# First layer's attention in fixed ticks, four projection blocks moved beside the memory, ten k-tiles of the output projection beside the attention

## Chip, cores and metric

One core of a Trainium2 chip runs the whole program in one launch. The metric is the device time of that launch in microseconds (us). TensorE (PE) multiplies and transposes, VectorE (DVE), ScalarE (ACT) and GpSimd (POOL) do the elementwise work, and SyncE (SP) issues nearly all DMAs from one queue. Each engine works through its own instructions in order and waits on semaphores for the others, so an instruction that waits also holds up everything behind it on its engine.

## The reference, cut to what matters

Two layers, 1280 tokens of width 1024 (1024 sample tokens, 256 prompt tokens). The first layer runs two mixers on one input projection:

```python
qa, ka, va, za, qb, kb, vb, ob, zb, gb = jnp.split(h @ w_in, AB_SPLITS, axis=-1)
# A: 16 heads on 4 key heads, window +-128 (sample) plus 256 cached keys, a sink logit per head
s_loc = jnp.einsum('bqhgd,bkhd->bhgqk', qi, ki) * scale      # 3 blocks of 128 keys, masked
s_ctx = jnp.einsum('bqhgd,bkhd->bhgqk', qi, ck) * scale      # 256 cached keys
p = jax.nn.softmax(jnp.concatenate([s_loc, s_ctx, sink_b], axis=-1), axis=-1)
a_out = attn * jax.nn.silu(za)
# B: matrix memory, chunkwise, both directions, 4 heads
hb, states = _mlstm_bidir(qb, kb, vb, ob, gb + gate_bias, conv_w, norm_w, init)
b_out = hb * jax.nn.silu(zb)
out = jnp.concatenate([a_out, b_out], axis=-1) @ w_out       # 16 k-tiles of 128
```

The second layer (latent attention) follows; the change does not alter what it computes.

## The kernel before, in words

Every matmul operand is split into a high and a low part (names ending in h and l), and each product is three matmuls: high by high, high by low, low by high. The first layer's input projection is cut into 30 blocks of 256 columns (`DenseBlock`). A block's weights come in four DMAs of two k-tiles each into `wf` (two buffers); `split` then casts each k-tile to `wh` on ACT (L350) and subtracts on POOL to get `wl` (L351). A block is about ten cost units of 24 matmuls each for 256 columns, two units for 512.

The order of the work is set in two ways. Outside a `manual_schedule` block a scheduler with a timing model orders each engine's instructions. Inside, the order is that of the code. `beside_memory` is of the second kind: the memory's work is cut into 80 visits of 2 slots each, 174 slots in all, and every slot issues the steps of `Visit.STEPS` for the visits that are due, then dense work up to a quota (`while spent * slots < (s + 1) * total`), then one call of `dense.pump`, which either asks for a DMA of the next block's weights or splits weights that came at least three slots after the last ask. When a block starts, `load` asks and splits at once whatever is still missing. Steps that must come later in the flow are put off by `K.later`.

The stages of the first layer: five blocks while the gates are made, 20 blocks beside the memory, then attention. Attention has 4 key groups `g` by 10 query blocks `b`. `a_attn` makes the scores of four heads in the PSUM tile `D`, takes the maximum on DVE, the exponential on ACT and the normalisation on POOL (`att_p`). `a_use` turns each block of 128 keys with four PE transposes into `T`, splits it into `att_ph` (ACT) and `att_pl` (DVE), and multiplies by the values into `V`. I call one key block of `a_use` a turn; there are 168. The first 21 of the 40 groups stand beside the last five dense blocks, the others beside `out_tile` of 9 token tiles, with 12 of the 16 k-tiles of the output projection (`woh`, `wol`, `o_ah`, `o_al`); a tenth token tile follows. The remaining 4 k-tiles come in a second pass, `wo2`, with the norm for the second layer.

Of the kernel before, what the change touches and what calls it, by code (L numbers as in the profile page):

```python
# [77 lines left out]
class Kern:  # L78
    def __init__(self, tc, I, O, dbg):
        self.tc, self.nc, self.I, self.O, self.dbg = tc, tc.nc, I, O, dbg  # L80
        self.uid = 0
        self.flow = self.ring = None

# [245 lines left out]
class DenseBlock:  # L329


    def __init__(self, K, wp, cols, fn, bufs, width, src="w_in_ab"):
        self.K, self.wp, self.cols, self.fn, self.bufs, self.width = K, wp, cols, fn, bufs, width
        self.src, self.w, self.wf, self.asked = K.I[src][0], [], [], 0
# [26 lines left out]
    def run(self):  # L361

        units = self.fn(self.w)
        if self.K.flow:
            for half in range(2):
                for u in units[0:2]:
                    u.products(half)
                    yield u.cost / 2
            units = units[2:]
        for u in units:  # L370
            for half in range(2):
                u.products(half)
                if half or u.cost > 1:
                    yield min(u.cost, 1)


class Unit:
# [8 lines left out]
    def products(self, half):  # L386
        K = self.K
        if not half:
            self.ps = K.ps()
        for k in range(half * KD // 2, (half + 1) * KD // 2):  # L390
# [4 lines left out]
        if half:  # L395
            self.done(self.ps)

# [24 lines left out]
class Dense:  # L422
# [162 lines left out]
def rope_split(K, pool, ps, t0, N, scale, dh, dl):  # L585
# [4 lines left out]
    nc.vector.tensor_mul(t, ps[:, 0:N], tab[:, 0, t0:t0 + N])  # L590
    nc.vector.stream_shuffle(s, ps[:, 0:N], ROT16)
    nc.gpsimd.tensor_mul(s, s, tab[:, 1, t0:t0 + N])

    def add():
        nc.vector.tensor_add(t, t, s)
        split_to(K, pool, t, 128, N, scale, dh, dl)

    K.later(add)
# [39 lines left out]
def layer_ab(K):  # L638
# [97 lines left out]

    K.set_psum(S=3, mm=3, T=2)
    bp = left("mls")
    with K.tc.manual_schedule():
        beside_memory(K, bp, dense, 20, 200)  # L740
    bp.release()
    K.set_psum(D=2, mm=1, V=1, T=2)
    ap = left("att")
    a_sinks(K, ap)
    attn = pipelined([a_attn(K, ap, g) for g in range(4)], 2)
    banks = itertools.cycle((partial(K.bank, "mm"), K.psT, K.psT))

    def beside(n):

        K.ps = lambda: next(banks)()  # L750
        for i, cost in enumerate(dense.stream(5)):
            if i == n:
                del K.ps
            yield cost

    weave(attn, 21, beside(10), 50, 0)
    K.rpool.release()
    tp.release()
    K.ring = None
    wp.release()  # L760
    hp.release()
    p = right("wo1")
    w = I["w_out_ab"][0]
    ks = [8, 9, 10, 11, 12, 13, 14, 15, 0, 1, 2, 3]
    wt = load_wout(K, p, w, ks)
    K.y1 = [K.t(K.dram, [128, D], F32, f"y1_{t}") for t in range(NT)]
    K.y2 = [K.t(K.dram, [128, D], F32, f"y2_{t}") for t in range(NT)]
    gate = gate_rows(K, p, 0)

    def first_part(tts):  # L770
        for tt in tts:
            srcs = [(d["bT"][tt], 0, 6), (d["bT"][tt], 6, 8, d["aT"][tt], 0, 4)]
            K.dma(K.y1[tt], out_tile(K, p, srcs, wt, gate[0 if tt < 8 else 1], x_src(K, tt), 6))
            yield 1

    weave(attn, 4 * NT + 1 - 21, first_part(range(9)), 9, 7)
    K.ps = lambda: next(banks)()
    for _ in first_part(range(9, NT)):
        pass
    p.release()  # L780
    ap.release()
    gp.release()
    del K.ps
    K.set_psum(S=5, T=3)
    p = left("wo2")
    wt = load_wout(K, p, w, range(4, 8))
# [10 lines left out]
    for tt in range(NT):  # L797
        if tt in (0, 8):
            gate = gate_row(K, p, 0, tt // 8)
        y = out_tile(K, p, [(d["aT"][tt], 4, 8)], wt, gate, K.y1[tt], 4, xb=2)  # L800
# [10 lines left out]
def load_wout(K, p, src, ks):  # L811

    nc = K.nc
    stage = [K.t(p, [128, D], F32, "o_y", 2) for _ in range(2)]
    out = [[p.tile([128, D], F32R, tag=f"{t}{i}", name=K.nm(t)) for t in ("woh", "wol")] for i in range(len(ks))]
    for i, (k, (wh, wl)) in enumerate(zip(ks, out)):
        wf = stage.pop(0) if stage else K.t(p, [128, D], F32, "o_y", 2)
        K.dma(wf, src[k * 128:(k + 1) * 128, :])
        nc.scalar.copy(wh, wf)
        (nc.gpsimd if i % 3 else nc.vector).tensor_sub(wl, wf, wh.bitcast(F32))  # L820
# [3 lines left out]
def out_tile(K, p, srcs, wt, gate, res, nk, each=None, xb=1, fast=False):  # L824
# [4 lines left out]
    y = K.t(p, [128, D], F32, "o_y", 2)  # L829
# [122 lines left out]
def a_attn(K, ap, g):  # L952
    nc, d = K.nc, K.d
    j, r = g // 2, (g % 2) * 64
    kk = []
    for nm in ("kh", "kl"):
        t = K.t(ap, [128, 1536], F32R, "att_" + nm, 1)
        for half in range(2):
            K.dma(t[half * 64:half * 64 + 64, :], d[nm][j][r:r + 64, :])
        kk.append(t)  # L960
    kkh, kkl = kk
    VA = K.t(ap, [128, 12, 128], F32R, "att_v", 1)
    K.dma(VA, d["vhl"][:, :, g, :].rearrange("i p d -> p i d"))
    for b in range(NT):
        ts_ = slice(b * 128, (b + 1) * 128)
        qs = K.t(ap, [128, 4, 128], F32R, "att_q", 2)
        for half, nm in enumerate(("qh", "ql")):
            K.dma(qs[half * 64:half * 64 + 64], d[nm][g][:, ts_].rearrange("(h d) t -> d h t", d=64))
        sz = K.t(ap, [128, 2, 128], F32, "att_z", 2)
        K.dma(sz, d["sza"][g][:, ts_].rearrange("(j p) t -> p j t", p=128))  # L970
        if b < 8:
# [1062 lines left out]
```

## Time and profile before

| | |
|---|---|
| median of 3 runs | 2681.3 us (2680.96 to 2682.63) |
| profiled execution, own time | 2685.41 us |
| its span, first to last instruction | 2683.5 us |
| PE busy / DVE / ACT / POOL in that span | 97% / 66% / 52% / 42% |
| mean granted TensorE clock | 0.989 |

The span is what the rows of the trace add up to; 1.9 us of the profiled execution lie outside it. PE is the engine that is nearly always busy, so what matters is where PE waits or runs at half clock. A row's PE busy time has each matmul's full latency, and matmuls overlap: a wait shorter than this overlap does not show as idle.

### The profile page before, as it was taken

How to read it: one execution, taken by the hardware profiler on the slowest of the kernel's cores; microseconds unless marked ns; L12 is line 12 of the kernel's file. 1: busy time of each engine (PE TensorE's matmuls, PEld its weight loads, DVE VectorE, ACT ScalarE, POOL GpSimd, SP SyncE). 2: the span in 40 equal slices, each digit the busy share in tenths (PEclk: the TensorE clock that was granted, in tenths of full speed). 3: DMA queues.
4: the chain of work that ended last, by engine and by line, in shares of the span. 5: the costliest groups of instructions: out<-in, count | busy, mean ns of one | idle time of the engine just before them, and what ended most of it. 6: DMA issues, size and time to landing. Idle time of an engine off the chain costs nothing.

```text
span 2683.5 us, 47955 instructions
## 1 busy us (share of the span) xinstructions
PE 2593.8 (97%) x16209; PEld 2267.6 (85%) x16209; DVE 1772.4 (66%) x4054; ACT 1393.9 (52%) x3558; POOL 1124.4 (42%) x1479
## 2 busy tenths in 40 slices
PE   8989999999999999999899999999899999999998
PEld 6878899898899887888688888987799999999887
DVE  6983565664764754665756637434788888888854
ACT  5222544434444334555654433332688888888842
POOL 4332433333333433443543336222455555545742
PEclk9989999999999999999999999999999999999999
DMA  7554576576586745342734356423311111100333
GB/s 246 176 163 147 163 210 203 140 226 199 152 236 188 218 134 132 103 118 77 225 99 127 93 169 197 146 70 117 117 30 35 37 31 36 40 21 27 120 103 128
DMA packets 340391, 348.77 MB, mean 130 GB/s; under 512 B 28489, under 2 KB 288246, under 8 KB 339890
## 3 DMA queue, kind: packets, MB, share of 16 engines
q1 hardware_dynamic: 340146, 345.71, 43.0%
q8 instruction: 129, 2.11, 0.3%
q14 instruction: 116, 0.95, 0.1%
HBM read 235.09 MB, written 110.51 MB: 129 GB/s over the span
## 4 chain that ended last, share of the span: by engine, by line
PE 57%; DMA 3%; DVE 2%; ACT 2%; POOL 1%; issue 1%; SPq 1%; DVEq 0%; POOLq 0%; ACTq 0%
PE S L100 20%; PE mm L100 16%; PE V L100 8%; PE T L104 8%; PE D L100 3%; PE T L100 1%; SPq L135 1%; DMA wf<-in_w_in_ab 1%; DMA wk<-in_w_kvb_c 1%; DMA o_y<-in_w_out_ab 0%; ACT att_p L1002 0%; DMA att_kl<-kl 0%; POOL wol L820 0%; DMA att_kh<-kh 0%; DMA aT<-att_z 0%
## 5 line engine op out<-in xcount | busy, mean ns | idle before, releaser
L351 POOL TENSOR_TENSOR wl<-wf,wh 128x256 fp32r<-128x256 f32 (+2 forms) x288 | 241.8, 864 | 403.3 <-ACT wh L350 330.8
L100 PE MATMUL mm<-hTh,wh 128*128 128x512 f32 (+1 forms) x880 | 320.3, 364 | 1.3 <-DVE bmod L303 0.8
L100 PE MATMUL mm<-hTh,wl 128*128 128x512 f32 (+1 forms) x880 | 316.7, 360 | 0.0
L100 PE MATMUL mm<-hTl,wh 128*128 128x512 f32 (+1 forms) x880 | 316.6, 360 | 0.0
L100 PE MATMUL S<-cK,cQ 96*128 96x512 f32 (+3 forms) x1248 | 298.1, 364 | 2.6 <-ACT cPb L1936 1.0
L1984 DVE TENSOR_TENSOR cpl<-T,cph 128x512 fp32r<-128x512 f32 x336 | 228.5, 685 | 40.8 <-ACT cph L1983 37.1
L100 PEld LDWEIGHTS S<-cK,cQ 96*128 96x128 f32 (+1 forms) x1248 | 192.4, 189 | 25.3 <-ACT cPa L1936 3.1
L1983 ACT CAST cph<-T 128x512 fp32r<-128x512 f32 x336 | 192.3, 589 | 31.6 <-PE T L104 19.3
L1007 POOL TENSOR_SCALAR att_p<-att_p,att_den 128x640 f32<-128x640 f32 (+2 forms) x160 | 115.3, 734 | 185.3 <-DVE att_den L1004 170.8
L100 PEld LDWEIGHTS mm<-hTh,wl 128*128 128x128 f32 x880 | 167.0, 190 | 26.4 <-POOL wl L351 0.3
L100 PEld LDWEIGHTS mm<-hTh,wh 128*128 128x128 f32 x880 | 167.0, 190 | 25.4 <-DVE bmod L303 1.7
L100 PEld LDWEIGHTS mm<-hTl,wh 128*128 128x128 f32 x880 | 167.0, 190 | 22.7
L1934 DVE TENSOR_REDUCE cmx<-S 128x1 f32<-128x512 f32 x256 | 172.8, 682 | 15.2 <-PE S L100 13.8
L100 PE MATMUL V<-cph,cV 128*128 128x256 f32 x672 | 177.0, 290 | 1.6 <-DVE co L1999 1.5
L350 ACT CAST wh<-wf 128x256 fp32r<-128x256 f32 (+2 forms) x288 | 103.5, 410 | 133.1 <-DMA wf<-in_w_in_ab 98.8
L100 PE MATMUL V<-cpl,cV 128*128 128x256 f32 x672 | 171.9, 284 | 0.2 <-DVE cpl L1984 0.2
L1002 ACT ACTIVATE att_p<-D,att_nm 128x641 f32<-128x641 f32 (+2 forms) x160 | 114.2, 715 | 88.0 <-PE T L104 32.9
L1915 POOL TENSOR_SCALAR cPa<-cPa,cst 128x512 f32<-128x512 f32 x128 | 100.9, 788 | 116.4 <-DVE cst L1912 91.1
L1021 DVE TENSOR_TENSOR att_pl<-T,att_ph 128x512 fp32r<-128x512 f32 x168 | 114.3, 687 | 47.9 <-ACT att_ph L1020 46.1
L100 PE MATMUL mm<-wh,hTh 128*128 128x256 f32 x480 | 138.6, 289 | 4.5 <-DVE scr L1228 2.4
L100 PE MATMUL mm<-wl,hTh 128*128 128x256 f32 x480 | 137.0, 285 | 3.1 <-POOL wl L351 2.8
L1020 ACT CAST att_ph<-T 128x512 fp32r<-128x512 f32 x168 | 96.7, 587 | 75.3 <-PE T L104 55.1
(441 smaller groups left out, 7968.1 us busy)
## 6 DMA issues: line engine op xcount, KB each, us to landing
wf<-in_w_in_ab SPq DMA_DIRECT2D x120, 256.0 KB
in<-in SPq DMA_DIRECT2D x40, 514.0 KB
in<-in SPq DMA_DIRECT2D x32, 386.0 KB
mw<-in_w_mod SPq DMA_DIRECT2D x48, 256.0 KB
in<-scr SPq DMA_DIRECT2D x40, 258.0 KB
y<-o_y SPq DMA_DIRECT2D x20, 512.0 KB
o_x<-y SPq DMA_DIRECT2D x20, 512.0 KB
wm<-in_w_mod SPq DMA_DIRECT2D x16, 512.0 KB
```

Of the source, the lines that this page charges most:

```text
L100: return self.nc.tensor.matmul(out, lhsT, rhs, start=start, stop=stop)
L104: self.nc.tensor.transpose(out, in_, self.ident[:p, :p])
L350: K.nc.scalar.copy(wh, wf[:, k])
L351: K.nc.gpsimd.tensor_sub(wl, wf[:, k], wh.bitcast(F32))
L1002: nc.scalar.activation(P[:, hi, off - 128:641], S[:, off:769], AF.Exp, bias=nm[:, hi:hi + 1], accum_out=den[:, hi:hi + 1])
L1007: nc.gpsimd.tensor_scalar(pv, pv, den[:, hi:hi + 1], 1.0, ALU.mult, ALU.mult)
L1020: nc.scalar.copy(ph, T_)
L1021: nc.vector.tensor_sub(pl, T_, ph.bitcast(F32))
L1915: nc.gpsimd.tensor_scalar(pv, pv, wt[:, c:c + 1], rd, ALU.mult, ALU.mult)
L1934: nc.vector.tensor_reduce(mx[:, b, c:c + 1], S, AX.X, ALU.max, negate=True)
L1983: nc.scalar.copy(ph, T_)
L1984: nc.vector.tensor_sub(pl, T_, ph.bitcast(F32))
```

## The change

Beside the memory the quota rises from 200 cost units (20 blocks) to 240 (24 blocks) over the same 174 slots. `pump` keeps a due slot for each asked piece of weights, and may ask and split in one slot. The attention leaves the scheduler: a class `Attention` sets a list of ticks, one turn per tick, one head's scores per tick, each at least four ticks ahead of the turn that needs it. Only one dense block is left, in the first 13 ticks. Then the dense pools are released, and the output projection's weights, ten k-tiles instead of twelve, are asked one per three ticks; its product steps (3 matmuls of 128x512) go in at one per three ticks, then some 1.2 per tick. 160 of 200 steps are so placed, the other 40 follow. The second pass has 6 k-tiles instead of 4. Keys and values of a group come in parts, each as soon as its place is free. In the attention all `wl` subtractions of the output weights stand on POOL, in halves.

```diff
     def pump(self, now):
+        if not self.blocks:
+            return
         b = self.blocks[0]
         if b.asked < KD // 2 and len(b.wf) < 2:
             b.ask()
-            b.when = now + 3
-        elif b.wf and len(b.w) < 2 * b.bufs - KD and now >= b.when:
+            b.when.append(now + 3)
+        if b.wf and len(b.w) < 2 * b.bufs - KD and now >= b.when[0]:
+            b.when.pop(0)
             b.split()
...
-        beside_memory(K, bp, dense, 20, 200)
-    bp.release()
-    K.set_psum(D=2, mm=1, V=1, T=2)
...
-    weave(attn, 21, beside(10), 50, 0)
...
-    ks = [8, 9, 10, 11, 12, 13, 14, 15, 0, 1, 2, 3]
...
-    weave(attn, 4 * NT + 1 - 21, first_part(range(9)), 9, 7)
...
+        beside_memory(K, bp, dense, 24, 240)
...
+        K.set_psum(D=2, mm=3, V=1)
+        ap = left("att")
+        a_sinks(K, ap)
+        steps = beside_attention(K, ap, dense, release)
...
+    wt = load_wout(K, p, w, range(2, 8))
+    for _ in steps:
+        pass
...
+class Attention:
+    ORDER = (0, 1, 2, 8, 3, 4, 5, 9, 6, 7)
+    LEAD = 12
...
+    def run(self, pump, extra):
+        K, flow = self.K, self.K.flow
+        for i in range(self.end + 5):
+            flow.now += 1
+            pump(flow.now)
+            for f in self.ask.get(i, ()):
+                f()
+            if i - 2 in self.score:
+                G, h = self.score[i - 2]
+                if h % 2:
+                    G.normal(h // 2)
+            if i - 1 in self.score:
+                G, h = self.score[i - 1]
+                G.peak(h)
+            if i in self.use:
+                G, k = self.use[i]
+                G.turn(k)
+                G.split(k)
+            if i - 1 in self.use:
+                G, k = self.use[i - 1]
+                G.weighted(k)
+                if k == len(G.kbs) - 1:
+                    G.out()
+            if i - 1 in self.score:
+                G, h = self.score[i - 1]
+                G.exp(h)
+            flow.step()
+            extra(i)
+            if i in self.score:
+                G, h = self.score[i]
+                G.scores(h)
...
+def beside_attention(K, ap, dense, release):
+    A = Attention(K, ap)
+    units, spent, steps, left = dense.units(1), 0, None, 160
+    lead = A.LEAD + 1
+    n = lead + 4
+    def extra(i):
+        nonlocal spent, steps, left
+        while spent < 10 and spent < max(3, (i + 1) * 10 / lead):
+            spent += next(units, 10)
+        if i == n:
+            steps = release()
+        while i > n + 8 and left > (160 - (i - n - 8) / 3 if i < n + 39 else 150 * (A.end - i) / (A.end - n - 39)):
+            next(steps)
+            left -= 1
```

`peak` is the sink copy and the maximum (DVE), `exp` the exponential (ACT), `normal` the normalisation (POOL), `turn` the four transposes, `split` the parts `att_ph` and `att_pl`, `weighted` the two products with the values; each does for one head or one key block what `a_attn` and `a_use` did. A layer-two scratch pool (`szp`), finer yields of a dense block and a common buffer ring for the weights of every output projection come with it.

Where the pieces of weights stand. SP before, at the start of a block beside the memory; the first `wf` is the fourth and last piece of the block that starts (`wf_1517`), the next two are the first two of the block after.

```order
L135 DMA in2_42_115<-scr_1498_7354 128x516
L135 DMA wf_1517_7427<-in_w_in_ab 128x2x256
L135 DMA wf_1528_7471<-in_w_in_ab 128x2x256
L135 DMA ho_1529_7473<-st1_45_118 128x256
L135 DMA tho_1530_7475<-st1_45_118 128x256
L135 DMA in2_42_115<-scr_1516_7423 128x516
L135 DMA wf_1538_7532<-in_w_in_ab 128x2x256
```

ACT before, in the same slot: the casts of `wf_1517` stand with no other slot's work between its ask and them, and the memory's `Ch`, `tho` and `hh` behind them.

```order
L1227 CAST scr_1516_7423<-mm_1499_7358 128x256
L350 CAST wh_1518_7429<-wf_1462_7187 128x256
L350 CAST wh_1520_7433<-wf_1462_7187 128x256
L350 CAST wh_1522_7437<-wf_1517_7427 128x256
L350 CAST wh_1524_7441<-wf_1517_7427 128x256
L1377 CAST Ch_1535_7499<-Cs_1046_5329 128x516
L1451 ACTIVATE tho_1465_7193,hss_1537_7504<-hh_1514_7417 128x256
L1459 ACTIVATE hh_1485_7284<-hh_1485_7284,hrs_1515_7419 128x256
```

SP after, at such a place: `wf_711` and `wf_729` are the third and fourth piece of a block, `wf_759` is the first piece of the one after and is asked in the slot in which the block starts.

```order
L138 DMA wf_711_3776<-in_w_in_ab 128x2x256
L138 DMA st0_44_117<-km_701_3725 128x256
L138 DMA st0_44_117<-ho_707_3740 128x256
L138 DMA in1_41_114<-cx_678_3615 128x4x128
L138 DMA wf_729_3846<-in_w_in_ab 128x2x256
L138 DMA wi_730_3848<-grow_52_125 128x128
L138 DMA sd0_48_121<-sd_721_3814 128x256
L138 DMA st0_44_117<-ho_737_3870 128x256
L138 DMA in1_41_114<-cx_708_3745 128x4x128
L138 DMA wf_759_3989<-in_w_in_ab 128x2x256
```

The fourth piece moved from the slot of the block's start to two or three slots ahead of it.

The attention on PE, after, in the ticks in which the output projection has begun (`mm` is both the turned tile and, by another number, the output sums):

```order
L107 MATMUL mm_3374_15878<-small_66,att_p_3300_15571 128x128 x2
L107 MATMUL mm_3374_15878<-small_66,att_p_3312_15627 128x128 x2
L103 MATMUL V_3361_15821<-att_ph_3364_15843,att_v_13973 128x512
L103 MATMUL V_3361_15821<-att_pl_3365_15844,att_v_13973 128x512
L103 MATMUL mm_3368_15857<-w_3084_14663,o_ah_3337_15727 128x512
L103 MATMUL mm_3368_15857<-w_3085_14664,o_ah_3337_15727 128x512
L103 MATMUL mm_3368_15857<-w_3084_14663,o_al_3338_15728 128x512
```

ACT after, in those ticks: per tick one `att_ph`, one `att_p`, and at times a half of an output weight between them.

```order
L819 CAST w_3105_14748<-w_3017_14435 128x512
L1129 CAST att_ph_3113_14775<-mm_3112_14770 128x512
L1109 ACTIVATE att_p_3109_14765,att_den_3111_14767<-D_3107_14753,att_nm_3110_14766 128x641
L819 CAST w_3105_14748<-w_3017_14435 128x512
L1129 CAST att_ph_3119_14810<-mm_3118_14805 128x512
L1109 ACTIVATE att_p_3109_14765,att_den_3111_14767<-D_3117_14792,att_nm_3110_14766 128x641
```

What moved: before, one cast of 1024 columns stood for these two, and the scheduler put several heads or turns together.

## Rows read from the trace of the kernel before

**Rows 1.** The page's first part: busy us, share of the span, instructions.

```profile
PE 2593.8 (97%) x16209; PEld 2267.6 (85%) x16209; DVE 1772.4 (66%) x4054; ACT 1393.9 (52%) x3558; POOL 1124.4 (42%) x1479
```

**Rows 2.** Busy by stretch: length, PE, PEld, DVE, ACT, POOL, clock, DMA, GB/s.

```profile
1400.00:1550.00 150.00, 149.99 (x835) 124.57 (x834) 88.64 (x185) 71.12 (x159) 51.48 (x61) 1.00 0.39 114
1584.00:1600.00 16.00, 16.00 (x72) 13.25 (x71) 5.79 (x6) 6.09 (x7) 7.93 (x4) 1.00 0.83 297
240.00:1008.00 768.00, 748.62 (x4901) 678.24 (x4901) 470.16 (x1245) 324.36 (x876) 283.66 (x358) 0.99 0.64 188
500.00:600.00 100.00, 94.61 (x676) 88.40 (x675) 68.13 (x188) 42.04 (x113) 39.03 (x49) 0.98 0.68 190
900.00:1000.00 100.00, 94.44 (x503) 80.44 (x502) 67.76 (x165) 33.44 (x88) 36.23 (x43) 0.95 0.57 176
1008.00:1578.00 570.00, 548.77 (x3140) 452.41 (x3139) 346.50 (x749) 293.38 (x662) 222.81 (x266) 0.99 0.42 121
1020.00:1040.00 20.00, 17.15 (x85) 13.83 (x85) 5.49 (x14) 4.71 (x12) 4.15 (x6) 0.91 0.63 162
1280.00:1320.00 40.00, 31.30 (x175) 23.77 (x173) 29.74 (x62) 28.89 (x60) 20.14 (x21) 0.91 0.95 274
1299.00:1345.00 46.00, 40.14 (x234) 30.24 (x232) 35.19 (x71) 35.88 (x69) 32.27 (x28) 0.96 0.70 207
1578.00:1700.00 122.00, 122.00 (x616) 103.00 (x615) 72.20 (x107) 44.64 (x84) 66.62 (x60) 1.00 0.56 183
```

**Rows 3.** Who PE waited for, 240 to 1008: us, times, longest.

```profile
PE T L104 <- ACT hh L1459: 6.1, 4, 3.1
PE mm L100 <- POOL wl L351: 2.8, 7, 0.4
...
PE mm L100 <- ACT wh L350: 2.0, 2, 1.5
```

**Rows 4.** Line L350 in 240 to 1008: idle of ACT before it.

```profile
  DMA wf<-in_w_in_ab: 47.5, 16
```

**Rows 5.** Timelines of SP, ACT and PE around 390: start, us, row [idle before].

```profile
388.56 1.77 SPq L135 DMA_DIRECT2D wf<-in_w_in_ab  x2
...
391.24 0.71 ACT L350 CAST wh<-wf 128x256 fp32r<-128x256 f32 x2 [3.29 <-DMA wf<-in_w_in_ab]
...
395.57 0.44 PE L104 MATMUL T<-small,hh 128*128 128x128 f32 x2 [1.82 <-ACT hh L1459]
```

**Rows 6.** PE groups, 1400 to 1550: count, busy us, mean ns.

```profile
L100 PE MATMUL mm<-woh,o_ah 128*128 128x512 f32 x123 | 49.8, 405 | 0.0
...
L100 PE MATMUL V<-att_pl,att_v 128*128 128x512 f32 x44 | 17.6, 399 | 0.0
```

**Rows 7.** PE groups, 1299 to 1345.

```profile
L100 PE MATMUL D<-att_kh,att_q 128*128 128x384 f32 (+1 forms) x34 | 13.8, 405 | 1.4 <-ACT att_p L1002 1.4
...
L100 PE MATMUL V<-att_ph,att_v 128*128 128x512 f32 x17 | 7.3, 431 | 1.6 <-DVE att_o L1029 1.6
```

**Rows 8.** Groups by shape, 1008 to 1578.

```profile
L1021 DVE TENSOR_TENSOR att_pl<-T,att_ph 128x512 fp32r<-128x512 f32 x168 | 114.3, 687 | 47.9 <-ACT att_ph L1020 46.1 <-PE mm L100 0.4
...
L1020 ACT CAST att_ph<-T 128x512 fp32r<-128x512 f32 x168 | 96.7, 587 | 75.3 <-PE T L104 55.1 <-PE V L100 18.9 <-DVE att_pl L1021 0.3
...
L1001 DVE TENSOR_REDUCE att_nm<-D 128x1 f32<-128x641 f32 x96 | 78.4, 821 | 2.1
L1007 POOL TENSOR_SCALAR att_p<-att_p,att_den 128x640 f32<-128x640 f32 x96 | 78.4, 830 | 78.0 <-DVE att_den L1004 67.3 <-PE D L100 4.7 <-PE V L100 3.3
L1002 ACT ACTIVATE att_p<-D,att_nm 128x641 f32<-128x641 f32 x96 | 76.9, 802 | 41.7 <-DVE att_nm L1001 22.1 <-DVE D L1000 13.4 <-PE T L104 3.2
...
L820 POOL TENSOR_TENSOR wol<-o_y,woh 128x1024 fp32r<-128x1024 f32 x8 | 19.0, 2379 | 5.4 <-ACT woh L819 5.2
```

**Rows 9.** Who PE waited for, 1008 to 1578: us, times, longest.

```profile
PE D L100 <- DMA att_kh<-kh: 3.5, 1, 3.5
PE D L100 <- DMA wf<-in_w_in_ab: 2.9, 1, 2.9
```

More of the change, by code (lines that the diff above doesn't have):

```diff
@@ L370, in run @@
         for u in units:
[L371 to L374, printed above, removed]
+            n = u.cost if self.K.pairs else 2 * u.cost
+            for i in range(n):
+                u.products(i, n)
+                yield u.cost / n
 class Unit:
@@ L384, in __init__, with products @@
         self.cost = 2 if self.n == 512 else 1
-    def products(self, half):
+    def products(self, part, n):
         K = self.K
-        if not half:
+        if not part:
             self.ps = K.ps()
-        for k in range(half * KD // 2, (half + 1) * KD // 2):
+        for k in range(part * KD // n, (part + 1) * KD // n):
             a, b = [t[:, self.fs:self.fs + self.F] for t in self.w[k]]
@@ L394, in products @@
                 K.mm(self.ps[0:128, 0:self.n], x, y, k + i == 0, k == KD - 1 and i == 2)
-        if half:
+        if part == n - 1:
             self.done(self.ps)
+            K.filled = K.flow and K.flow.now
 def unit_T(K, w, fs, ci, done):
@@ L737, in layer_ab @@
     K.set_psum(S=3, mm=3, T=2)
     bp = left("mls")
+    K.flow = Flow()
     with K.tc.manual_schedule():
-        beside_memory(K, bp, dense, 20, 200)
-    bp.release()
-    K.set_psum(D=2, mm=1, V=1, T=2)
[L743 to L754, printed above, removed]
@@ L756, in layer_ab @@
-    weave(attn, 21, beside(10), 50, 0)
[L757 to L763, printed above, removed]
-    ks = [8, 9, 10, 11, 12, 13, 14, 15, 0, 1, 2, 3]
[L765 to L774, printed above, removed]
@@ L813, in load_wout, with split, begin, ask @@
     nc = K.nc
[L814 to L818, printed above, removed]
-        nc.scalar.copy(wh, wf)
-        (nc.gpsimd if i % 3 else nc.vector).tensor_sub(wl, wf, wh.bitcast(F32))
+    K.wbufs = 2 * len(ks) + (1 if len(ks) == 6 else 2)
+    out = []
+    def split(i, wf, half=None):
+        wh, wl, wf = [t if half is None else t[:, half * 512:half * 512 + 512] for t in (*out[i], wf)]
+        nc.scalar.copy(wh, wf)
+        (nc.gpsimd if K.flow or i % 3 else nc.vector).tensor_sub(wl, wf, wh.bitcast(F32))
+    def begin(i, wf):
+        out.append([K.t(p, [128, D], F32R, "w", K.wbufs) for _ in range(2)])
+        if K.flow:
+            split(i, wf, 0)
+            K.later(partial(split, i, wf, 1))
+        else:
+            split(i, wf)
+    for i, k in enumerate(ks):
+        wf = K.t(p, [128, D], F32, "w", K.wbufs)
+        def ask(i=i, k=k, wf=wf):
+            K.dma(wf, src[k * 128:(k + 1) * 128, :])
+            K.later(partial(begin, i, wf), 4)
+        K.later(ask, 1 + 3 * i)
     return out
@@ new lines, in beside_attention @@
+def beside_attention(K, ap, dense, release):
[10 more added lines that the diff above has]
+        while i > n + 8 and left > (160 - (i - n - 8) / 3 if i < n + 39 else 150 * (A.end - i) / (A.end - n - 39)):
+            next(steps)
+            left -= 1
+    A.run(dense.pump, extra)
+    K.flow.drain()
+    return steps
```

314 lines of the change are left out of this document (220 added, 94 removed).

## The prediction

> **What bounds the kernel now.** I read the page's busy times first [rows 1]: PE is busy 97% of the span, the next engine 66%. So the time is PE's own work plus what PE loses, and since the change neither adds nor drops a product (it moves 4 blocks and 2 k-tiles to other stages), only the losses can change. Then I read busy times by stretch [rows 2]. In 1400 to 1550 PE is busy 149.99 of 150 us and the clock is 1.00, with the same mix of attention and output projection: this is what the kernel does where nothing is late. In 1584 to 1600 only the output projection's matmuls of 512 columns run, 72 in 16.0 us, so one costs 0.225 us from start to start (16.0 / 71), although its row says about 0.4 us [rows 6]: the latencies overlap, and waits of up to 0.17 us per matmul hide in "busy". The beside-memory stage (240 to 1008) has 768 us with PE busy for 748.6: 19.4 us idle. The attention (1008 to 1578) has 570.0 with 548.8: 21.2 us idle. On top comes the clock. It stands at 0.98 in 500 to 600 and 0.95 in 900 to 1000, which is 2 + 5 = 7 us lost to its 1.2 GHz level in the first stage; at 0.91 in 1020 to 1040 and 0.91 in 1280 to 1320, 1.8 + 3.6 = 5.4 us in the second. In the latter two stretches PE had been idle 2.9 and 8.7 us. So 26.4 us are lost in each of the two stages to be seen, and more is hidden in busy time.
>
> Then I asked who PE waits for. Beside the memory it is the cast of `hh` on ACT (6.1 us in 4 waits), the weights' low part `wl` on POOL (2.8 us) and their high part `wh` on ACT (2.0) [rows 3]. One cause stands behind most of these: ACT itself sits idle 47.5 us in 16 waits for the DMA of `wf` before it can cast it [rows 4], about one wait per block. The timeline around 390 shows one [rows 5]: SP issues two `wf` from 388.56, ACT is idle 3.29 us until 391.24 for one of them, all of ACT's memory work stands behind that cast, and at 395.57 PE has waited 1.82 us for `hh`. In the attention PE waits longest for the keys of a new group, `att_kh` (3.5 us), and at its beginning for a `wf` (2.9) [rows 9]; each is followed by the half clock above.
>
> **The change part by part.** *Weights beside the memory.* Why is the last piece late? By the code before, each new ask moves the one due slot back three slots, and a slot asks or splits, so a block's pieces are asked at slots 0, 1 and 5 and the fourth only when the block starts, in slot 8 or 9; it is then split at once. A DMA that was asked in the same slot holds ACT until it lands. After the change a piece has its own due slot: counted through the code the asks come in slots 0, 1, 4 and 5 and the block starts in slot 7 or 8, so the last piece has two to three slots. A slot of before is 768 / 174 = 4.4 us and the new one longer, so at least 9 us, against waits of 3 us on average (47.5 / 16) and 3.29 us in the one shown. Price: of the 19.4 us of idle time I count the 10.9 of `hh`, `wl` and `wh` as gone and, my choice, 5 of the remaining 8.5, since most of PE's other waits also end in something that ACT or DVE did late; with the 7 us of clock, which fell after such waits, this is 23 us. From below, only the direct waits on weights go: 2.8 + 2.0 = 5 us. From above, all 26.4 go and as much as the clock's 7 us hides in busy time: 33 us. I take 23.
>
> *Four more blocks in the same 174 slots.* A block is 96 matmuls of 512 and 48 of 256 columns: 96 x 0.225 + 48 x 0.113 (half the columns, half the price, an estimate) = 27 us. So the stage grows by 108 us of PE work to some 768 - 23 + 108 = 853 us, 4.9 us a slot. The other engines have room: DVE was busy 470 of 768 us, ACT 324, POOL 284 [rows 2]; with the extra weights and rotary steps none comes near 853. I cost it at nothing; if the rotary steps on DVE hold the PSUM tiles as they may, it costs 2 to 5 us. What the 108 us add here they take from the attention.
>
> *The attention in ticks.* PE's own price of a tick: in 1400 to 1550 there are 3 x 123 product matmuls, 369 x 0.225 = 83 us, and 44 turns with their heads [rows 6], so (150 - 83) / 44 = 1.52 us per turn. The after-time in four pieces. (a) Opening, 13 ticks: one dense block, 27 us, and the first eight heads, 8 x 0.6 = 5: 32 us. 0.6 us per head is what is left of 1.52 us after four transposes and two products of 512 columns. (b) Some 43 light ticks, until the weights are there: PE has 1.52 us plus at first nothing, then a third of a product step (0.23 us). Here PE can't be the bound alone. Per tick DVE does a maximum and a low part, 0.821 + 0.687 = 1.51 us, ACT a high part and an exponential, 0.587 + 0.802 = 1.39, POOL a normalisation, 0.830, and a third of an output k-tile, 2.379 / 3 = 0.79, so 1.62 [rows 8]. Nothing below 1.65 us a tick is thus to be had: 71 us. The nearest row from above is 1299 to 1345, where the scheduler ran attention beside the loading weights: 46 us for 17 turns and 17 heads [rows 2, 7], 2.7 us each: 116 us. The new order has one head and one turn in every tick and leaves two ticks between normalisation and turn, so I take 2.0 us, nearer to the sums: 86 us. (c) 124 steady ticks with 1.21 steps of 3 x 0.225 us: 1.52 + 0.82 = 2.34 us each, 290 us, PE-bound by a margin of 0.8 us over DVE's 1.51, plus 5 us where the three `mm` banks are held by an output sum, its successor and a turned tile at once. (d) 40 steps after the last turn, 120 x 0.225 = 27 us. Sum: 32 + 86 + 290 + 5 + 27 = 440 us. The same work before: 1008 to 1600 is 592 us, less the four blocks (108) and less two k-tiles of ten token tiles (120 x 0.225 = 27) that go to the second pass: 457. The attention gains 17 us; with the ends of (b), 32 to a loss of 13.
>
> *Parts of keys, own `wf` for the opening.* The waits of 3.5 and 2.9 us and their clock are in these 17 us: the parts are asked as their place comes free, ticks ahead.
>
> *Second pass.* Its six k-tiles load behind piece (d), 27 us of matmuls, where four loaded behind 16 us; a tile now has 36 matmuls (8.1 us) instead of 24 (5.4) while its elementwise work per tile is nearly unchanged, and PE was busy 122.0 of 122 us there [rows 2]. Cost nothing; without that cover it is 5 us. *The rest* (layer-two scratch pool, finer yields, common ring for output weights, which lets the last projection's weights be asked earlier): the scheduler orders that part anew; 0, plus or minus 3 us.
>
> Sum: 23 + 17 = 40 us. The profiled execution took 2685.4 us (2683.5 of span and 1.9 outside), 4.1 us over the median, inside 0.2%; its difference carries over to the median: 2681.3 - 40 = 2641 us.
>
> **Rivals.** *The weights aren't the cause.* The stalls beside the memory come from the memory's own chain, and move when the weights come in time. For it: only 4.8 us of PE's waits name weights. Against it: [rows 5], and that the waits come one per block. Then 5 us are gained there: 2681.3 - 5 - 17 = 2659. *The light ticks run at the scheduler's pace*, 2.7 us: 30 us more than I count, 2671. For it: the three elementwise engines hand a tile round twice per tick, in order; against it: in 1299 to 1345 whole k-tiles of 2.4 us stood in POOL's way, now halves.
>
> *The other side: the tick is a chain.* In a tick PE's transposes wait for POOL, ACT for PE, DVE for ACT, PE's products for DVE, and each engine's later work stands behind. If this chain takes 2.7 us also in the 124 steady ticks, which were to take 2.34, they cost 45 us more, with (b) 75: 2716, slower. It decides from about 2.42 us per steady tick on if (b) is at 2.7 as well: 30 + 124 x 0.08 = 40. Against it: a steady tick has 0.8 us of product steps between one turn's transposes and the products that need them, which a light tick lacks.
>
> *Half clock in the light ticks.* In 1299 to 1345 PE idled 5.9 of 46 us and the clock was at 0.96, so it was at 1.2 GHz for some 3.7 us [rows 2]; in the 43 light ticks PE would idle about 0.35 us in each. If it spent them at 1.2 GHz, PE would need 2 x 1.65 = 3.3 us a tick instead of 2.0: 56 us more, 2697. A rule of the Trainium skill speaks for this: "TensorE: Matmul & The Clock Gate", section "A second HAM failure mode: psum-queue depth-cycling", tells of a kernel whose brief idle spells between groups of matmuls made the clock go up and down. By that rule the change would be slower; the trace agrees only in part, since most of that stretch ran at 2.4 GHz.
>
> **How the numbers follow.** Both gains as counted 0.62, weights not the cause 0.12, light ticks at the scheduler's pace 0.12, the chain 0.07, half clock 0.04, better than the ends 0.03. The likeliest gives 2641. Its own range: memory 5 to 33, attention from a loss of 13 to 32 us, rarely both at one end: 2616 to 2663. To leave out no more than 2 in 10 the range takes in the two middle rivals: 2614 to 2671. Less than 0.2% (5.4 us) is what a measurement can't tell from no change. Faster needs a time under 2676: the main case, most of both middle rivals: 0.85. The chain and the clock give slower 0.09. 0.06 stays for the same.
>
> **What would show it.** ACT's wait for `wf` beside the memory falls from 47.5 us to under 5 with no wait of 3 us at the blocks' starts, and the stage ends near 1093 with no clock fall. If the wait is gone and PE's idle time is still near 20 us, the first step is wrong. The last turn comes near 1093 + 413 = 1506. Turns 2.0 us apart at the start of the attention and 2.3 later show the second step; 2.7 in either shows the rival. A granted clock under 0.9 over the light ticks shows the last one. PE busy throughout from the last turn to the second layer's projections shows the cover. The prediction fails if a DMA in SP's single queue stands behind a wait and the keys or queries come late, of which the rows of before show nothing.

## The result, and the profile after

The changed kernel takes 2660.2 us (median of 4 runs, 2656.9 to 2662.1) against 2681.7 of the kernel before on the same chip: a ratio of 0.9918, 95% interval 0.9901 to 0.9936, 21.5 us faster where 40 were predicted. A second set of runs gave 0.9914 (0.9900 to 0.9927). The spans of the two profiled executions are 2659.5 and 2683.5 us, 24.0 apart; the accounts below are of these.

The page's first part after, against [rows 1]:

```profile
PE 2584.5 (97%) x16209; PEld 2264.8 (85%) x16209; DVE 1775.5 (67%) x4040; ACT 1409.0 (53%) x3598; POOL 1167.7 (44%) x1533
```

PE is still the bound, so again only its losses count. Busy by stretch in the changed kernel (columns as in [rows 2]), cut where its stages end: the memory at 1087, the first turn's products at 1122, the 43rd turn at 1211, the last turn at 1507, the second layer's attention from 1891.

```profile
240.00:1087.00 847.00, 845.14 (x5467) 763.83 (x5466) 509.94 (x1299) 347.62 (x930) 323.43 (x396) 1.00 0.61 185
1087.00:1122.00 35.00, 34.20 (x195) 29.18 (x196) 11.22 (x26) 10.31 (x25) 7.12 (x10) 1.00 0.51 152
1122.00:1211.00 89.00, 78.51 (x498) 62.71 (x496) 74.09 (x167) 73.74 (x169) 64.06 (x75) 1.00 0.60 179
1211.00:1507.00 296.00, 290.86 (x1740) 242.46 (x1739) 220.92 (x478) 192.00 (x438) 144.99 (x188) 1.00 0.36 106
1507.00:1891.00 384.00, 368.81 (x1930) 315.50 (x1929) 172.42 (x336) 122.69 (x273) 139.80 (x139) 0.97 0.44 139
1507.00:1660.00 153.00, 149.95 (x712) 122.73 (x711) 71.09 (x116) 49.55 (x95) 73.66 (x65) 1.00 0.51 164
1660.00:1700.00 40.00, 36.80 (x222) 36.33 (x221) 16.03 (x35) 7.24 (x17) 5.22 (x6) 0.91 0.61 208
1830.00:1891.00 61.00, 52.07 (x277) 43.79 (x276) 43.31 (x78) 28.29 (x59) 28.58 (x27) 0.89 0.55 170
```

Beside the memory PE now idles 1.9 of 847 us at a clock of 1.00, where it idled 19.4 of 768 at 0.99 [rows 2]. The losses have moved to the end of this list: 15.2 us idle between the last turn and the second layer's attention, and clock falls at 1660 and at 1830.

ACT's casts of `wf` beside the memory, 240 to 1087, as a group (busy, mean ns, idle before it and its causes), against [rows 4]:

```profile
L353 ACT CAST wh<-wf 128x256 fp32r<-128x256 f32 x188 | 65.2, 406 | 4.2 <-PE mm L103 3.7 <-DMA wf<-in_w_in_ab 0.4
```

The 47.5 us for the DMA are 0.4. Who PE waited for in the same stretch, against [rows 3]:

```profile
PE mm L103 <- DVE bmod L306: 0.8, 1, 0.8
PE mm L103 <- POOL wl L354: 0.5, 2, 0.3
PE T L107 <- DVE um L1575: 0.3, 1, 0.3
```

The waits for `hh`, 6.1 us before, are gone; in `b_pump` below, which touches nothing of the memory's own chain, 1.9 us of them are left.

In the attention, 1087 to 1507, against [rows 9]:

```profile
PE V L103 <- DVE att_o L1148: 12.2, 29, 1.1
PE V L103 <- DVE att_pl L1130: 2.3, 8, 0.5
```

The keys and the `wf` are gone from the list. What is left stands ahead of the first product of a group: the sums V of a group lie in one PSUM bank, and two operations on ACT and two on DVE read it before the next group may write it. One such place, from the timeline at 1164 (start, us, row [idle before]):

```profile
1163.67 0.38 ACT L1145 ACTIVATE att_o<-V 64x256 f32<-64x256 f32 x1
...
1164.07 0.38 ACT L1146 ACTIVATE att_o<-V 64x256 f32<-64x256 f32 x1
...
1164.53 0.41 DVE L1147 SCALAR_TENSOR_TENSOR att_o<-V,att_o 64x256 f32<-64x256 f32 x1
...
1164.96 0.43 DVE L1148 SCALAR_TENSOR_TENSOR att_o<-V,att_o 64x256 f32<-64x256 f32 x1
...
1165.54 0.47 PE L103 MATMUL V<-att_ph,att_v 128*128 128x512 f32 x1 [0.92 <-DVE att_o L1148]
```

From 1163.67 to 1165.39 the four read one after the other, and the product, for which PE has idled 0.92 us, starts 0.15 us behind the last.

From the last turn to the second layer's attention, 1507 to 1891:

```profile
PE S L103 <- DVE cK L1823: 3.7, 1, 3.7
PE S L103 <- ACT wh L353: 3.2, 1, 3.2
PE S L103 <- DVE rp_s L570: 2.0, 2, 1.6
PE T L107 <- DVE cq L1826: 1.7, 2, 1.0
PE S L103 <- ACT wr L1878: 1.4, 1, 1.4
```

The `wh` (3.2 us, up to 1671.3) belongs to the second block of the second layer; its `wf` was issued at 1660.69.

**The account.** A block moved beside the memory costs 27.5 us of PE: 845.14 here less 735.17 in the same stage with 20 blocks (the row of the first experiment), by four. The four are 110 us, and two k-tiles 27 as in the prediction. The first output pass ends at 1601 in the trace of before and at 1534 here, the second layer's attention begins at 1915 and 1891.

| stage (us) | before | after | work moved | gained |
|---|---|---|---|---|
| beside the memory, from 240 | 766 | 847 | +110 | 29 |
| attention and first output pass | 595 | 447 | -110 - 27 | 11 |
| second pass, second layer's projections | 315 | 357 | +27 | -15 |
| second layer's attention to the end | 768 | 769 | 0 | -1 |

The sum is 24 us, the difference of the spans. So the two stages that were rebuilt gave the 40 us that were predicted, and 15 of them were lost behind them.

### The profile page after: what moved, and what is told of

It is laid out like the page before. It is cut to its first block, busy times and chain, and to the rows that moved or that the text cites. A ratio compares the mean times of both kernels' runs of the same rounds, so it can differ in the third digit from the quotient of the medians.

```text
span 2659.5 us, 48212 instructions
## 1 busy us (share of the span) xinstructions
PE 2584.5 (97%) x16209; PEld 2264.8 (85%) x16209; DVE 1775.5 (67%) x4040; ACT 1409.0 (53%) x3598; POOL 1167.7 (44%) x1533
## 5 line engine op out<-in xcount | busy, mean ns | idle before, releaser
L354 POOL TENSOR_TENSOR wl<-wf,wh 128x256 fp32r<-128x256 f32 (+2 forms) x288 | 251.7, 899 | 455.0 <-ACT wh L353 385.1
L103 PE MATMUL mm<-hTh,wh 128*128 128x512 f32 (+1 forms) x912 | 328.3, 360 | 1.6 <-DVE scr L620 0.9
L103 PE MATMUL mm<-hTl,wh 128*128 128x512 f32 (+1 forms) x912 | 325.1, 356 | 0.0
L103 PE MATMUL mm<-hTh,wl 128*128 128x512 f32 (+1 forms) x912 | 325.0, 356 | 0.0
L103 PE MATMUL S<-w,o_ah 128*128 128x512 f32 x492 | 151.8, 395 | 1.7 <-POOL w L820 0.8
L103 PE MATMUL mm<-w,o_ah 128*128 128x512 f32 x468 | 148.6, 396 | 0.0
L1129 ACT CAST att_ph<-mm 128x512 fp32r<-128x512 f32 x168 | 98.6, 587 | 93.8 <-PE mm L107 92.5
L1118 POOL TENSOR_SCALAR att_p<-att_p,att_den 128x640 f32<-128x640 f32 (+1 forms) x128 | 97.5, 775 | 108.9 <-DVE att_den L1115 47.9
L1130 DVE TENSOR_TENSOR att_pl<-mm,att_ph 128x512 fp32r<-128x512 f32 x168 | 115.8, 689 | 33.1 <-ACT att_ph L1129 27.9
```

The costliest lines, as they stand in the source:

```text
L103: return self.nc.tensor.matmul(out, lhsT, rhs, start=start, stop=stop)
L354: K.nc.gpsimd.tensor_sub(wl, wf[:, k], wh.bitcast(F32))
L1118: nc.gpsimd.tensor_scalar(pv, pv, den[:, i:i + 1], 1.0, ALU.mult, ALU.mult)
L1129: K.nc.scalar.copy(ph, self.T)
L1130: K.nc.vector.tensor_sub(pl, self.T, ph.bitcast(F32))
```

## The experiments

**The rule of the pump alone, and everything but that rule.** In the kernel before, `b_pump` has only this edit; in the changed kernel, `a_oldpump` takes it back:

```diff
-        self.src, self.w, self.wf, self.asked = K.I[src][0], [], [], 0
+        self.src, self.w, self.wf, self.when, self.asked = K.I[src][0], [], [], [], 0
...
-            b.when = now + 3
-        elif b.wf and len(b.w) < 2 * b.bufs - KD and now >= b.when:
+            b.when.append(now + 3)
+        if b.wf and len(b.w) < 2 * b.bufs - KD and now >= b.when[0]:
+            b.when.pop(0)
             b.split()
```

> The kernel before with one edit of the change alone: a due slot for each piece of the weights, and a slot may ask for one piece and split another. Theory (late weights make the stalls beside the memory): the time falls by 20 to 27 us against the kernel before, to 2655 to 2662 us; ACT's wait for wf beside the memory falls from 47.5 us to under 5 and the stage (240 to 1008 us before) ends some 20 to 27 us sooner. Rival (the memory's own chain makes them): only the 5 us of waits that name weights go, 2676 us, and PE's idle time in the stage stays above 14 us.

> The changed kernel with the old rule of the pump (one due slot, a slot asks or splits). Theory: the 28 to 30 us that the stage beside the memory gained by my reading of the two traces are this rule's, so the time rises by 25 to 30 us, to 2685 to 2690 us, and ACT again waits 40 us or more for wf there. Rival: in the longer slots (4.9 us instead of 4.4) the last piece comes in time anyway, and less than 10 us are lost (under 2670 us).

`b_pump`: 2661.3 us, ratio 0.9903 (0.9889 to 0.9916). `a_oldpump`: 2692.8 us, 1.0027 (1.0017 to 1.0037), slower than the kernel before. The stage beside the memory in `b_pump`, as a stretch and then ACT's casts in it:

```profile
240.00:981.00 741.00, 735.17 (x4892) 670.02 (x4891) 473.21 (x1242) 325.06 (x878) 286.08 (x360) 1.00 0.66 194
```

```profile
L350 ACT CAST wh<-wf 128x256 fp32r<-128x256 f32 x160 | 55.1, 406 | 5.8 <-PE mm L100 5.8
```

The same two of `a_oldpump`, the stretch cut where the memory ends and the row of the casts taken to 1119; then the first long wait of PE behind the memory and the stretch around it:

```profile
240.00:1111.50 871.50, 855.55 (x5467) 766.37 (x5466) 494.61 (x1299) 345.25 (x927) 313.98 (x394) 1.00 0.59 179
```

```profile
L353 ACT CAST wh<-wf 128x256 fp32r<-128x256 f32 x190 | 65.5, 405 | 82.2 <-DMA wf<-in_w_in_ab 80.7 <-PE mm L103 1.5
```

```profile
1123.00 0.80 PE L103 MATMUL mm<-hTh,wh 128*128 128x512 f32 x1 [5.95 <-ACT wh L353]
```

```profile
1112.00:1126.00 14.00, 7.42 (x25) 5.54 (x26) 0.61 (x2) 2.08 (x8) 4.25 (x6) 0.76 0.51 147
```

Both theories hold, the second with a little more than said: the stage ends 25 us sooner with the rule (981 against 1006), and 25 us later without it (1111.5 against 1087). The other 7 us of `a_oldpump` lie right behind, in the dense block beside the opening of the attention, whose weights come by the same rule: PE waits 5.95 us for a `wh`, and the clock around it is 0.76. The rivals fall; longer slots don't help, since ACT's wait grows to 80.7 us. And one thing follows that was not expected: this edit of four lines is the whole gain. All the rest of the change loses 0.2 to 0.4% with the old rule and is worth nothing with the new one (0.9903 against 0.9918 and 0.9914, with overlapping intervals).

**The bank of V.** One copy frees it, and the rest works from SBUF:

```diff
-        nc.scalar.mul(o[0:64], v[64:128, :, 0, :], 0.5)
-        nc.scalar.mul(o[64:128], v[0:64, :, 1, :], 0.5)
-        nc.vector.scalar_tensor_tensor(o[0:64], v[0:64, :, 0, :], 0.5, o[0:64], ALU.mult, ALU.add)
-        nc.vector.scalar_tensor_tensor(o[64:128], v[64:128, :, 1, :], 0.5, o[64:128], ALU.mult, ALU.add)
+        c = K.t(self.A.ap, [128, 512], F32, "att_c", 1)
+        nc.scalar.mul(c, self.av, 0.5)
+        c = c.rearrange("p (j r t) -> p j r t", j=2, r=2)
+        nc.scalar.copy(o[0:64], c[64:128, :, 0, :])
+        nc.scalar.copy(o[64:128], c[0:64, :, 1, :])
+        nc.gpsimd.tensor_add(o[0:64], o[0:64], c[0:64, :, 0, :])
+        nc.gpsimd.tensor_add(o[64:128], o[64:128], c[64:128, :, 1, :])
```

> The changed kernel, with the bank of the attention's sums V freed by one copy on ACT (halved, to SBUF), from which two copies on ACT and two additions on POOL then make the group's output; before, two operations on ACT and two on DVE read the bank itself. Theory: PE's wait ahead of the first product of each group (some 40 of them, 20 us in all in the trace of after) is for this bank, so most of it goes and the time falls by 10 to 16 us, to 2644 to 2650 us. Rival: PE then waits as long for what ACT or POOL do late, since both have more work at the group's end, and the time is within 3 us of the changed kernel.

2654.4 us, ratio 0.9879 (0.9864 to 0.9894). The attention, from the memory's end to the last turn, takes 412.2 us instead of 420.0. PE's waits in 1123 to 1500:

```profile
PE D L103 <- ACT att_p L1109: 4.0, 6, 0.9
PE mm L107 <- POOL att_p L1118: 1.8, 3, 1.1
PE V L103 <- DVE att_pl L1130: 1.6, 6, 0.3
PE D L103 <- ACT att_pp L1109: 0.5, 1, 0.5
PE V L103 <- ACT att_c L1144: 0.3, 1, 0.3
```

The bank's wait falls from 12.2 to 0.3 us; 6.3 us of new waits come, for the exponential on ACT and the normalisation on POOL, on the engines that took work over. The theory holds below its range by the spans (7 us) and at its lower end by the ratio (10 us). The 20 us of its text were counted from the spacing of PE's starts; the profile names 12.2.

**A block's products in the light ticks.** 23 blocks beside the memory and two beside the opening, over 26 ticks; the output weights are released 13 ticks later in `a_two`, 12 in `a_two12`:

```diff
-        beside_memory(K, bp, dense, 24, 240)
+        beside_memory(K, bp, dense, 23, 230)
...
-    units, spent, steps, left = dense.units(1), 0, None, 160
+    units, spent, steps, left = dense.units(2), 0, None, 160
...
-    n = lead + 4
+    n = lead + 4 + 13
...
-        while spent < 10 and spent < max(3, (i + 1) * 10 / lead):
-            spent += next(units, 10)
+        while spent < 20 and spent < max(3, (i + 1) * 20 / (lead + 13)):
+            spent += next(units, 20)
```

> The changed kernel with 23 blocks beside the memory and two beside the opening of the attention, whose products are spread over the first 26 ticks, so that 13 of the ticks that were light have a block's products in them and the output projection's weights are released 13 ticks later. Theory: in the 43 light ticks (1.86 us each against PE's own 1.52) PE idles some 0.3 us per tick, and products put there cost less: the time falls by 3 to 8 us against the changed kernel. Rival: the 50 product steps that leave the light ticks' tail make the steady ticks fuller, which are bound by PE anyway, and the time is within 3 us of the changed kernel; if the steady ticks can't take them, up to 6 us slower.

> The second dense block beside the opening, with the output projection's weights released 12 ticks later instead of 13. Theory: with 13, the loads of the release stood in SP's queue ahead of a group's queries, PE waited 5.2 us for them and ran at the lower clock after it; one tick earlier they miss each other, and the time is within 3 us of the changed kernel or up to 4 us faster. Rival: the transfers themselves collide, whatever the tick, and the loss of some 10 us stays.

`a_two`: 2675.7 us, 0.9961 (0.9947 to 0.9975). `a_two12`: 2671.8 us, 0.9949 (0.9937 to 0.9961). Both are slower than the changed kernel, `a_two` by more than the 6 us of its rival (11 by the spans). In `a_two` the largest wait of the light ticks is new (waits of PE in 1122 to 1210), and the clock falls behind it (busy by stretch):

```profile
PE D L103 <- DMA att_q<-ql: 5.2, 1, 5.2
```

```profile
1160.00:1170.00 10.00, 3.84 (x23) 2.97 (x22) 4.47 (x12) 4.06 (x10) 3.88 (x5) 0.79 1.05 314
1170.00:1180.00 10.00, 9.00 (x47) 7.16 (x45) 7.14 (x19) 8.03 (x21) 6.56 (x8) 0.87 0.64 176
```

SP issued the released loads (gate, rest of the sum, output weights), and the queries of the group ahead among them, from 1157.4 to 1163.8, before the queries that PE waited for (1164.58 and 1166.28), and the DMA engines are full (share 1.05). Late queries behind other loads in SP's one queue are what the prediction named as a way to fail. One tick earlier, in `a_two12`, the wait is 1.9 us in two, and the stage's loss is smaller but doesn't go, as its rival said: from the memory's end to the last turn it takes 452.6 us, 27.5 for the block and 425.1, against 420.0. The theory that idle time in the light ticks can be filled is not borne out; DVE and ACT are busy there for 74 of 89 us each, and the product steps taken from there have to be done in the steady ticks. How much of the remaining loss is these and how much the crowded queue was not separated. A further part lies elsewhere: in all three runs with 23 blocks PE waits beside the memory for a tile that it doesn't wait for in the changed kernel (waits of PE in `a_two12`, 240 to 1064), and the block taken away shortens that stage, counted from its first transposes, by some 24 us and not by 27.5.

```profile
PE mm L103 <- DVE scr L1440: 4.0, 3, 2.9
```

**The start of the second layer.** First the queue. In the trace of after SP stood 21.4 us at a store of the second layer's gate, with later loads behind it; here those stores go out from ACT's queue:

```diff
-    K.later(lambda: K.dma(dst, th if len(dst.shape) == 2 else th.rearrange("p (c t) -> p c t", t=128)))
+    K.later(lambda: (K.dma_act if tag == "sz2" else K.dma)(dst, th if len(dst.shape) == 2 else th.rearrange("p (c t) -> p c t", t=128)))
...
-            silu2_out(K, K.szp, ps, N, d["sz"][2 * z + j][:, t0:t0 + N])
+            silu2_out(K, K.szp, ps, N, d["sz"][2 * z + j][:, t0:t0 + N], "sz2")
```

> The changed kernel with the stores of the second layer's gate (csz) issued from ACT's queue in place of SP's. In the trace of after SP stands 21.4 us at such stores, with the loads of rotary tables, convolution weights and the next weights behind them, one of which PE waits for at 1667.8 us. Theory: this is what made the second layer's start some 15 us longer than counted, and the time falls by 5 to 12 us, to 2648 to 2655 us; SP's wait for sz_th is gone and no PE wait for in_w_in_c is left. Rival: the loss is the scheduler's new order of that part, and the time is within 3 us of the changed kernel.

2663.7 us, 0.9913 (0.9900 to 0.9927): the theory falls. PE's waits in 1537 to 1894:

```profile
PE S L103 <- DVE cK L1823: 4.4, 1, 4.4
PE S L103 <- ACT wr L1878: 3.3, 1, 3.3
PE S L103 <- DVE sz L645: 2.7, 2, 2.5
```

The wait for `wh` is gone, as foreseen, and others are there in its place.

Then the weights: a third staging tile. `a_wf3` gets its room from one load tile less in the second pass, `a_vw` is that with V's copy, `a_comb` with the second dense block too, `a_tri` is V's copy and the third tile with the second pass in three parts of two k-tiles (the last of these edits is not in it; it has its own, further down):

```diff
+        self.stage = 3 if src == "w_in_c" else 2
...
-        wf = K.t(self.wp, [128, 2, self.width], F32, "wf", 2)[:, :, 0:F]
+        wf = K.t(self.wp, [128, 2, self.width], F32, "wf", self.stage)[:, :, 0:F]
...
-            if self.asked < KD // 2 and len(self.wf) < 2:
+            if self.asked < KD // 2 and len(self.wf) < self.stage:
...
-        a = K.t(p, [128, nk, 128], F32, "o_a", 2)[:, 0:n, :]
+        a = K.t(p, [128, nk, 128], F32, "o_a", 1 if K.wbufs == 13 else 2)[:, 0:n, :]
```

> The changed kernel with a third staging tile for the second layer's projection weights, so that all four pieces of its second block are in SBUF before the first block ends (the room comes from one load tile less in the second output pass). Theory: of the 13 us that PE loses more than before between the second output pass and the second layer's attention, the 3.4 us wait for wh at 1667.8 us and the some 3 us at the 1.2 GHz clock behind it are this piece's, so 5 to 7 us are gained. Rival, as moving the gate's stores off SP's queue has shown: another wait is next in line (the banks freed by sz on DVE), and the time is within 3 us of the changed kernel.

> The third staging tile and the one copy of the sums V together. Theory: the two lie in different stages and add up, 7 us of V's copy (its span against the changed kernel's) and 5 to 7 of the staging tile: 12 to 14 us faster than the changed kernel, a ratio to the kernel before of about 0.986. Rival: the staging tile gives nothing, and the ratio is that of the copy alone, 0.988.

> The same two with the second dense block beside the opening of the attention as well. If that block alone is worth 3 to 8 us, the ratio to the kernel before is about 0.984; if it is worth nothing, 0.986 to 0.988.

`a_wf3`: 2669.6 us, 0.9942 (0.9928 to 0.9955). `a_vw`: 2655.9 us, 0.9889 (0.9876 to 0.9903), its rival, the copy alone. `a_comb`: 2670.2 us, 0.9944 (0.9931 to 0.9957), slower than either of its two forecasts: the loss of the second block once more. Busy by stretch in `a_wf3`, against the rows of 1507 and 1660 above:

```profile
1507.00:1660.00 153.00, 143.88 (x640) 113.26 (x639) 67.10 (x101) 44.26 (x82) 66.39 (x60) 0.99 0.49 161
1660.00:1700.00 40.00, 38.69 (x252) 36.87 (x251) 22.83 (x52) 11.74 (x28) 8.98 (x10) 1.00 0.64 219
```

From 1660 on the wait and the lower clock are gone, but the second pass loses 6 us more, 5.3 of them waiting for `o_ah` of the one load tile. The edit's own cost hides what it gives, so the next one pays for the room in another way; it also gives `o_ah` and `o_al` three buffers instead of two.

```diff
-        y = out_tile(K, p, [(d["aT"][tt], 2, 5), (d["aT"][tt], 5, 8)], wt, gate, K.y1[tt], 3)
+        y = out_tile(K, p, [(d["aT"][tt], a, a + 2) for a in (2, 4, 6)], wt, gate, K.y1[tt], 2)
```

> The changed kernel once more, unchanged, as the measure for the two below on the same chip: a ratio to the kernel before of 0.990 to 0.994, as in the first comparison (0.9918).

> The one copy of V and the third staging tile, whose room now comes from splitting each tile of the second output pass into three parts of two k-tiles (two load tiles stay) instead of two parts of three with one load tile. Theory: the one load tile cost what the staging tile gave (7 to 8 us of waits in the second pass against some 8 us at 1660 to 1700), so both gains show now: 5 to 7 us faster than the copy of V alone, a ratio of 0.985 to 0.986. Rival: the second pass loses again, by the nine more pairs of casts and loads, and the ratio stays at 0.988.

`a_again`: 2661.8 us, 0.9914 (0.9900 to 0.9927). `a_tri`: 2659.1 us (2648.8 to 2662.2), 0.9893 (0.9874 to 0.9911), not better than V's copy alone: the theory falls. Its trace has PE busy for 40.00 of 40 us in 1660 to 1700, at a clock of 0.97, and still takes 383.0 us from the last turn to the second layer's attention, against 384.0 in the changed kernel.

Last, the output tiles of the second pass: two in flight, as before the change, with V's copy and the same three parts.

```diff
-    K.wbufs = 2 * len(ks) + (1 if len(ks) == 6 else 2)
+    K.wbufs = 2 * len(ks) + 2
```

> The one copy of V, and a ring of 14 instead of 13 tiles for the second output pass, so that two output tiles can be in flight beside the twelve weight tiles as before the change (the room comes from three parts of two k-tiles per token tile). Theory: the single spare tile of the new ring makes weights and output tiles of the second pass wait, and is the cause of the some 11 us that PE loses more between the last turn and 1660 us than it did before: 5 to 8 us faster than the copy of V alone (a ratio of 0.985 to 0.986), with no wait for w at the pass's start. Rival: it is the order in which the scheduler puts the first projection's and the second block's products, which the tile doesn't change: ratio 0.987 to 0.989, PE's losses in this stretch as before within 3 us.

2654.0 us, 0.9879 (0.9862 to 0.9895), as V's copy alone: the rival. The stretch takes 384.6 us. In all twelve traces with the new attention (the changed kernel twice, ten with an edit) it lies between 382.2 and 387.9 us. The code before, with two k-tiles less, takes 338.6 in `b_pump`; with 27 us for them and 2 more for steps left after the last turn that makes 368. Some 15 us are thus lost in a way that none of the three suspects accounts for alone: the queue, the late piece and the single output tile were each taken away, other waits came in their place (2.5 us for `sz` in `a_csz`, 2.8 for `w` in `a_tri`, 3.0 for `o_ah` and 2.2 for `wh` in the last one), and the stretch kept its length. All three at once were not tried.

The traces do show where the loss lies. From the last turn to the end of the second layer's projections, at 1830, the changed kernel takes 322.9 us and the kernel before 279.2, to which the 29 us are to be added: 15 us. Behind that, with the waits for `cK`, `rp_s`, `cq` and `wr`, it takes 61 us and took 60. Of the 15, 6.3 are idle time of PE (3.05 in 1507 to 1660 and 3.2 in 1660 to 1700, by the rows above) and 3.6 the clock (40 x 0.09); before, PE waited for nothing in that stretch. The other 5 are spread over rows that count as busy.

One difference remains in the traces: in `b_pump` PE begins the second block's products at 1661.4, among those of the first, which end at 1673.2; in the changed kernel, as in all twelve, it begins them right behind the first's last (1659.6), and there a late piece stops it. Whether this order, which the scheduler chose, is the cause was not tried and stays open.

No version beat V's copy alone; it and the last one are the fastest, 0.9879.

## Why the prediction was right, and where it was not

**Weights beside the memory** (23 us counted, 5 to 33): right, 29 us measured. ACT's wait fell to 0.4 us, the clock is 1.00, the stage ends at 1087 where 1093 was said. With 20 blocks the same rule gives 25. Only 4.8 us of PE's waits had named weights, so the larger part came another way, and as argued: with the pump alone changed, PE's idle time falls from 19.4 to 5.8 us and its wait for `hh`, which stood behind the casts on ACT, from 6.1 to 1.9. No row divides the 29 us further. The first rival (the weights are not the cause, 2659 us) named the time that came, by another mechanism: `b_pump` shows that it isn't this one.

**Four more blocks for nothing**: right with the new rule (1.9 us idle in 847). With the old one they cost nothing more either: the stage of `a_oldpump` is 105.5 us longer than before (871.5 against 766), and the work moved is 110.

**The attention in ticks**: pieces of 32, 86, 295 and 27 us were said; 35.7, 88.8, 295.5 and 27.2 were measured (to the first turn's products, 43 turns, 124 turns, the steps left): 447 instead of 440. A light turn takes 2.07 us and a steady one 2.38, against 2.0 and 2.34. The last turn came at 1506.7, where 1506 was said, but through two errors that cancel: the memory ended 6 us sooner, the attention took 7 longer. The 17 us are thus 11. The 295 of the steady ticks came out with some luck: 5 of them were for the `mm` banks, and PE waited for none there; the waits that the profile names in 1211 to 1507, 4.8 us, are for V's bank. Not foreseen was V's bank, 12.2 us of waits, of which the copy got 8 back.

**The rivals of the tick.** Neither the chain nor the scheduler's pace came; 2.7 us per turn were to be seen in them. Half clock didn't either: PE idles 10.5 of 89 us in the light ticks and the granted clock is 1.00, its upper level of 2.4 GHz. The Trainium skill ("TensorE: Matmul & The Clock Gate", section "A second HAM failure mode: psum-queue depth-cycling") tells of a kernel in which brief idle spells between groups of matmuls made the clock go up and down, and that was weighed for this; the light ticks, with 19 waits of at most 1.1 us, don't agree with it. Elsewhere short waits did bring the clock down (last section).

**The second pass and the rest at nothing, plus or minus 3**: the step that failed, by 15 us, and the reason that the gain is 24 and not 40. The cover was there where it was named: 27 us of matmuls ran while the six k-tiles loaded, and PE then waited 1.6 us for their parts. What the term left out lies behind these waits, as far as the profile names it, up to the end of the second layer's projections. A part of the program that the scheduler orders anew was costed by its edits, which are small, and nothing was put on the order that comes out. Two thirds of the loss are waits and clock that the kernel before did not have there. What brings them, the new order or several causes at once, was not shown and stays open.

## What to carry to other kernels

An in-order engine that casts what a DMA brings must not be given the cast in the slot that issues the DMA (25 us of 2683 here): give every transfer a due time of its own, and look for the waits of others that stand behind the cast. When a change has one cheap part and one large one, run the cheap one alone first; here four lines gave as much as the whole. A stretch that a scheduler orders anew is not free because its edits are small: put a price or a wide range on it; here it cost 15 us, and taking the waits away one by one did not bring them back.

## What the runs showed that was not expected

Neither the length nor the number of PE's waits settles whether its clock falls. After 3.2 us of waiting up to 1671.3 it was granted 0.66 in 1670 to 1680; after 5.2 us in `a_two` 0.79 and 0.87; in 1830 to 1840, where PE idled 2.05 of 10 us, 0.83. In the light ticks, 10.5 us idle of 89 in pieces of up to 1.1 us, it stayed at 1.00:

```profile
1670.00:1680.00 10.00, 8.73 (x38) 8.53 (x39) 7.29 (x15) 3.68 (x9) 3.91 (x4) 0.66 0.83 265
1830.00:1840.00 10.00, 7.95 (x36) 6.06 (x35) 4.65 (x7) 6.16 (x11) 4.95 (x5) 0.83 0.73 188
```

In `a_csz` PE waited 2.5 us for `sz` at 1666, and in the 10 us from there the clock was 1.00:

```profile
1666.00:1676.00 10.00, 7.54 (x49) 7.54 (x50) 6.87 (x15) 4.29 (x10) 4.56 (x5) 1.00 0.81 252
```

So a single wait of that length did not bring it down there. And three waits of 0.2 to 0.4 us, between 1656 and 1659, are all that `a_tri` shows in the 10 us up to one fall: 1.1 us idle of 10, and a clock of 0.83. Waits of the same kind and length, between 1653 and 1656, left the changed kernel's at 1.00. First `a_tri`, then the changed kernel:

```profile
1655.00:1665.00 10.00, 8.89 (x50) 7.64 (x49) 5.17 (x12) 5.41 (x13) 4.66 (x6) 0.83 0.45 138
1650.00:1660.00 10.00, 8.71 (x63) 7.53 (x62) 6.42 (x14) 5.31 (x12) 2.98 (x4) 1.00 0.29 75
```

What tells these cases apart was not tried.
